# Cross-entropy backward on one core: blocks moved as even and odd partitions instead of row by row

## The chip, the core and the metric

The kernel runs on one core of a Trainium2 chip. The time is device microseconds of one execution; before the change the median of three runs is 1247.4 us (1247.38 to 1247.5).

Of the core, this case uses two compute engines, VectorE (DVE in the profile) and ScalarE (ACT), the queues that SyncE (SP) and ScalarE have for issuing DMAs, and the 16 DMA engines which move the data between the chip's main memory (HBM) and the on-chip memory with its 128 partitions (SBUF). TensorE and GpSimd work for a few microseconds at the start alone.

## The reference

```python
logits: (8, 1024, 8192) float32,  labels: (8, 1024) int32

logits_max = np.max(logits, axis=-1, keepdims=True)
exp_logits = np.exp(logits - logits_max)
softmax = exp_logits / np.sum(exp_logits, axis=-1, keepdims=True)
one_hot[batch_idx, seq_idx, labels] = 1.0
return (softmax - one_hot).astype(np.float32)
```

There are 8192 rows of 8192 numbers. 268 MB are read and 268 MB are written.

## The kernel before, in words

**Tiling.** The 8192 rows are cut into 32 blocks of 256 rows (8 MB). In a block, partition p holds the rows 2p and 2p + 1 of the block, side by side (lines 38 and 39). The two rows of one partition lie next to each other in HBM too: together they are one run of 64 KB, and one of them alone is a run of 32 KB. The code calls the first rows of all partitions j = 0 and the second ones j = 1; "row t" is row j = t % 2 of block t // 2, a tile of 128 partitions x 8192 numbers (4 MB). There are 64 such rows.

**Storage.** The tile X (line 45) has three slots of one block each, 192 KB in each partition. Block b lives in slot b % 3, from its load to its store; all work is done in place. So the load of block b has to wait until block b - 3 is stored.

**Work on a row** (loop of lines 160 to 190). VectorE takes the negated maximum (`row_max`, line 149). ScalarE computes exp(x - max) in place and the sum on the way. VectorE takes the reciprocal of the sum. ScalarE scales the row by it. VectorE subtracts the one-hot, by comparing a row of running numbers with the label (scalar_tensor_tensor, line 186). The order on VectorE is written out by hand: reciprocal of row t, maximum of row t + 1, subtraction of row t. So a row is finished only behind the maximum of the next row, and the last row of a block only after the first maximum of the next block. On ScalarE the order is: exp of row t, the issue of the store of row t - 1 (line 173), scaling of row t. Only the last row of all is scaled and finished in two pieces (lines 175 and 176).

**Transfers.** All loads are issued from SyncE's queue (`load`, line 120), all stores from ScalarE's (`store`, line 132). How a block moves is set by one letter for each block in two strings, LOADS and STORES (lines 13 and 14), and the table PIECES (line 105):

- "r": by row, two DMAs, each on all 128 partitions with runs of 32 KB;
- "w": whole, one DMA on all 128 partitions with runs of 64 KB;
- "h": two DMAs, one on the 64 even partitions and one on the 64 odd ones, both rows, runs of 64 KB.

Each DMA has its own semaphore for its slot and number (lines 58 and 59). A load waits for those stores of block b - 3 that share partitions and rows with it (`meets`, line 111, and line 125). A maximum waits for those loads of its block that have a part of its row (line 151): with "r" one load, with "w" and "h" the whole block. A store is issued with the last row that it holds (line 137): with "r" each row has its own, with "h" both DMAs go out with row j = 1.

Before the change, the loads of blocks 0 to 4 and 26 to 31 are "r" and those of blocks 5 to 25 are "w"; all stores are "r".

All operations are recorded by one helper, `run` (line 63), so the profile shows most of them as line 68.

Of the kernel before, what the change touches and what calls it, by code (L numbers as in the profile page):

```python
# [9 lines left out]
SLOTS = 3  # L10


LOADS = "rrrrrwwwwwwwwwwwwwwwwwwwwwrrrrrr"
STORES = "rrrrrrrrrrrrrrrrrrrrrrrrrrrrrrrr"


@with_exitstack
def kernel(
# [37 lines left out]
    with tc.tile_critical():  # L56
# [63 lines left out]
        def load(b):  # L120
            loaded[b] = []
            before = stored.get(b - SLOTS, last_made if b == SLOTS - 1 else [])
            for q, piece in enumerate(PIECES[LOADS[b]]):
                ps, js = piece
# [7 lines left out]
        def store(t):  # L132
            b, j = divmod(t, G)
            stored.setdefault(b, [])
            for q, piece in enumerate(PIECES[STORES[b]]):
                ps, js = piece
# [88 lines left out]
```

## Time and profile before

| | |
|---|---|
| median of three runs | 1247.4 us (1247.38 to 1247.5) |
| span of the profiled execution | 1245.7 us |
| the profiled execution beyond its span | not in the page; the median lies 1.7 us above the span |
| VectorE busy | 1119.2 us, 90% |
| ScalarE busy | 919.1 us, 74% |
| moved by the DMAs | 536.98 MB, mean 431 GB/s |
| maximum of a row (VectorE) | 64 of 8675 ns |
| subtraction of a row (VectorE) | 63 of 8743 ns |
| exp, and scaling, of a row (ScalarE) | 7123 ns each |
| store of a row, issue to landing | 64, median 30.8 us |
| load of a row, issue to landing | 22, median 26.6 us |
| load of a whole block, issue to landing | 21, median 33.4 us |

The profile is one execution on the chip, as the hardware profiler saw it. It has a page with the busy time of each engine, the span in 40 slices, the DMA queues and the chain of work that ended last, and further views that are asked for one by one: the list of waits, the chain in order of time, the instructions in a stretch of time, the busy times in given windows. Times inside the execution are counted from the start of the span. The trace also has a record for each DMA packet, with its queue, size, start and duration. A packet is one run of a DMA, 32 KB or 64 KB here; each of the 16 engines ends its part of a DMA with a packet of 4 bytes that reports it. A row's DMA gives each engine 8 packets.

In the DMA part, "q1" is the queue of the loads and "q10" that of the stores and of the labels; the columns are packets, MB, and the time that the packets took as a share of 16 engines' span.

### The profile page before, as it was taken

Reading aid. Unit: us, or ns where it says so; the run is one execution under the profiler, and the core shown is the slowest. Engines: PE = TensorE matmul, PEld = TensorE weight load, DVE = VectorE, ACT = ScalarE, POOL = GpSimd, SP = SyncE. Lnnn points to the kernel's source line nnn. Section 1 sums busy time; section 2 is a strip of 40 time slices with the busy share of each in tenths; the row PEclk is TensorE's granted clock in tenths of the full one; section 3 lists DMA queues with packets and bytes.
Section 4 is the critical chain, followed back from the end, with each engine's and each line's share of the span. In section 5 each row is a group of like instructions: output and inputs, shape, how many; then the busy total and the mean of one; then the engine's idle time right before and its main releaser. Section 6 shows DMA issues by size and latency. Waiting matters only on the chain.

```text
span 1245.7 us, 592 instructions
## 1 busy us (share of the span) xinstructions
PE 0.4 (0%) x2; PEld 0.3 (0%) x2; DVE 1119.2 (90%) x196; ACT 919.1 (74%) x194; POOL 7.4 (1%) x7
## 2 busy tenths in 40 slices
PE   0000000000000000000000000000000000000000
PEld 0000000000000000000000000000000000000000
DVE  5999998888988889888998888988889999999893
ACT  3888886778776787767877778777777788887772
POOL 2000000000000000000000000000000000000000
DMA  9999999999999999999999999999999999999998
GB/s 406 417 429 433 438 433 442 437 426 427 430 435 445 439 417 442 426 430 437 432 443 438 420 435 432 430 437 450 420 426 437 436 428 432 437 435 429 432 437 386
DMA packets 15460, 536.98 MB, mean 431 GB/s; under 512 B 1728, under 2 KB 1728, under 8 KB 1760
## 3 DMA queue, kind: packets, MB, share of 16 engines
q1 hardware_dynamic: 6192, 268.44, 50.0%
q10 hardware_dynamic: 9264, 268.51, 49.9%
q14 instruction: 4, 0.03, 0.0%
HBM read 268.50 MB, written 268.44 MB: 431 GB/s over the span
## 4 chain that ended last, share of the span: by engine, by line
DMA 59%; DVE 37%; another core or an unknown queue 2%; ACT 1%; DVEq 0%; issue 0%; PE 0%; SPq 0%; ACTq 0%
DMA X<-in_logits_dram 31%; DMA out_dram<-X 27%; DVE m L68 18%; DVE X L68 18%; ACT X L68 1%; DVE iota L68 0%; DVEq L56 0%; DMA lab_raw<-in_labels_dram 0%; DVE lab_f L68 0%; DVE r L68 0%; PE iota L68 0%; SPq L68 0%; ACTq L68 0%; DVE lab L68 0%
## 5 line engine op out<-in xcount | busy, mean ns | idle before, releaser
L68 DVE TENSOR_REDUCE m<-X 128x1 f32<-128x8192 f32 x64 | 555.2, 8675 | 94.3 <-DMA X<-in_logits_dram 94.3
L68 ACT ACTIVATE X<-X,m 128x8192 f32<-128x8192 f32 x64 | 455.9, 7123 | 188.4 <-DVE m L68 188.4
L68 DVE SCALAR_TENSOR_TENSOR X<-iota,lab,X 128x8192 f32<-128x8192 int16 (+1 forms) x65 | 559.7, 8612 | 4.1 <-ACT X L68 4.1
L68 ACT ACTIVATE X<-X,r 128x8192 f32<-128x8192 f32 (+1 forms) x65 | 456.0, 7017 | 115.9 <-DVE r L68 115.9
L68 DVE RECIPROCAL r<-s 128x1 f32<-128x1 f32 x64 | 9.9, 154 | 7.3 <-ACT X L68 7.3
L68 ACT ACTIVATION_READ_ACCUMULATOR X<-X,m 128x1 f32 x64 | 12.0, 187 | 0.0
L68 DVE CAST lab_f<-lab_raw 32x256 f32<-32x256 int32 x1 | 3.7, 3685 | 4.7 <-DMA lab_raw<-in_labels_dram 4.7
L68 POOL IOTA X<- 128x8192 int16 x1 | 6.9, 6944 | 0.0
L68 DVE TENSOR_SCALAR iota<-X 128x4096 int32<-128x4096 int32 x1 | 4.4, 4427 | 0.1
L68 ACT ACT_TABLE_LOAD x1 | 1.3, 1283 | 1.3 <-SPq L56 1.3
L68 DVE COPY lab<-iota 128x64 f32<-128x64 f32 x1 | 0.2, 225 | 0.5 <-PE iota L68 0.5
L68 PE MATMUL iota<-ident,lab_f 32*128 32x32 f32 x2 | 0.4, 300 | 8.5 <-DVE lab_f L68 8.5
L68 PEld LDWEIGHTS iota<-ident,lab_f 32*128 32x128 f32 x2 | 0.3, 196 | 8.4 <-DVE lab_f L68 8.4
L68 POOL TENSOR_SCALAR_AFFINE_SELECT ident<-ident 32x32 f32<-32x32 f32 x1 | 0.2, 204 | 0.1
L68 POOL MEMSET ident<- 32x32 f32 x1 | 0.1, 115 | 0.5 <-SPq L56 0.5
L209 POOL MEMSET const-bfloat16-1.0<- 128x1 bf16 x1 | 0.1, 107 | 0.0
L209 POOL MEMSET const-uint8-127<- 128x1 uint8 x1 | 0.1, 107 | 0.0
L209 POOL MEMSET const-float32-0.0<- 128x1 f32 x1 | 0.1, 104 | 0.2 <-issue 0.2
L209 POOL MEMSET const-float32-1.0<- 128x1 f32 x1 | 0.1, 104 | 0.0
## 6 DMA issues: line engine op xcount, KB each, us to landing
out_dram<-X ACTq DMA_DIRECT2D x64, 4096.0 KB, 30.8
X<-in_logits_dram SPq DMA_DIRECT2D x22, 4096.0 KB, 26.6
X<-in_logits_dram SPq DMA_DIRECT2D x21, 33.4
lab_raw<-in_labels_dram ACTq DMA_DIRECT2D x1, 64.0 KB, 3.8
```

Source lines behind the costliest of these rows:

```text
L68: instruction = getattr(engine, method)(**operands)
L209: nc = _bacc.Bacc("TRN2", target_bir_lowering=False, num_devices=1)
```

## The change

Two lines change. The loads of blocks 5 to 28 and the stores of blocks 2 to 25 become "h". The load of block b and the store of block b - 3, which use the same slot, are then cut in the same way: the load of the even partitions waits for the store of the even partitions alone, and that of the odd ones for the odd ones alone. The loads of blocks 0 to 4 and 29 to 31 and the stores of blocks 0, 1 and 26 to 31 are "r".

```diff
-LOADS = "rrrrrwwwwwwwwwwwwwwwwwwwwwrrrrrr"
-STORES = "rrrrrrrrrrrrrrrrrrrrrrrrrrrrrrrr"
+LOADS = "rrrrr" + "h" * 24 + "rrr"
+STORES = "rr" + "h" * 24 + "rrrrrr"
```

The functions that read the strings are unchanged. The number of DMAs goes from 43 loads and 64 stores to 64 loads and 64 stores, the bytes stay the same.

## The prediction

> **What bounds the kernel now.** I read the page's second and third parts first: the slices and the DMA queues.
>
> ```profile
> DMA  9999999999999999999999999999999999999998
> GB/s 406 417 429 433 438 433 442 437 426 427 430 435 445 439 417 442 426 430 437 432 443 438 420 435 432 430 437 450 420 426 437 436 428 432 437 435 429 432 437 386
> DMA packets 15460, 536.98 MB, mean 431 GB/s; under 512 B 1728, under 2 KB 1728, under 8 KB 1760
> ...
> q1 hardware_dynamic: 6192, 268.44, 50.0%
> q10 hardware_dynamic: 9264, 268.51, 49.9%
> ```
>
> The 16 DMA engines are busy in every slice, and the two queues (q1 the loads, q10 the stores) add up to 99.9% of 16 engines' span. VectorE (DVE) is at 90%, ScalarE (ACT) at 74%. The windows (us, busy time of PE, PEld, DVE, ACT and POOL, clock, DMA share, GB/s) say the same by stage:
>
> ```profile
> 0.00:46.00 46.00, 0.42 (x2) 0.28 (x2) 33.38 (x7) 22.84 (x6) 7.43 (x7) 1.00 0.97 412
> ...
> 300.00:500.00 200.00, 0.00 (x0) 0.00 (x0) 179.17 (x32) 147.76 (x33) 0.00 (x0) 1.00 1.00 434
> ...
> 1200.00:1246.00 46.00, 0.00 (x0) 0.00 (x0) 26.05 (x5) 19.83 (x5) 0.00 (x0) 1.00 0.92 398
> ```
>
> Only the two ends lose anything: the packet records show data from 2.15 us to 1244.2 us without an idle engine between. The list of waits agrees: VectorE waits for data, not the other way round, and these waits cost nothing by themselves.
>
> ```profile
> DVE m L68 <- DMA X<-in_logits_dram: 94.3, 25, 6.9
> ```
>
> So the time is the length of the packets. The records have one duration for each size, in both queues and at any time after the first microseconds: 1213 ns for 32 KB, 2418 ns for 64 KB, 9 ns for the small packet with which each engine ends a DMA. Each starts where the one before it ends, so no fixed cost hides between them. A 64 KB run is 2 x 1213 - 2418 = 8 ns cheaper than two of 32 KB.
>
> The chain of waits in order of time (start, us, what) shows one turn of the ring of three slots:
>
> ```profile
> 133.53 26.18 DMA out_dram<-X
> 159.71 0.02 issue
> 159.72 32.61 DMA X<-in_logits_dram
> 192.34 0.02 issue
> 192.36 8.69 DVE m L68
> 201.05 8.66 DVE X L68
> 209.71 0.03 DVE r L68
> 209.74 27.34 DMA out_dram<-X
> ```
>
> A store lands, the load into its slot is issued at once, the reduction of the new block starts when all of it is there, and the row before is finished behind that reduction (8.69 + 8.66 = 17.35 us after the landing). The chain shares (DMA 59%, DVE 37%) must not be read as two bounds: while VectorE stands in the chain, the engines are full with other blocks.
>
> **The change part by part.**
>
> 1. Packets. For each engine, before: 64 stores and 22 row loads of 8 packets of 32 KB, 688, and 21 whole loads of 8 packets of 64 KB, 168; 688 x 1.213 + 168 x 2.418 = 1240.8 us. After: 32 row DMAs (10 + 6 loads, 4 + 12 stores) of 8, 256, and 96 half DMAs of 4 packets of 64 KB, 384; 256 x 1.213 + 384 x 2.418 = 1239.0. That is -1.73 us. The queue shares check the size: 49.9% of 16 x 1245.7 over 8192 packets is 1.214 us.
>
> 2. Ending packets. DMAs of X go from 43 + 64 to 64 + 64: 21 more per engine at 9 ns, +0.19 us. Net -1.54 us.
>
> 3. Length of a packet that serves every second partition. The trace has no DMA on 64 partitions. Nothing below: the 8 ns are all that is fixed in a packet, so 384 packets can save at most another 3.1 us. Above, the nearest row in size is the whole load, 2.418 us, always. The only DMA on fewer partitions is that of the labels (32, packets of 2 KB: 81 to 315 ns, median 98), but the first packets of X on 128 partitions beside it are stretched as well (1.37 to 2.11 us for 1.213), so it shows the start and no price of partitions. I take 2.418.
>
> The row to weigh is that 128-partition DMAs keep 434 GB/s and both queues share them packet by packet. [...]
>
> 4. Stores wait for both rows of their block. The store of an even row is issued 17.3 us later than now, behind the odd row. It costs nothing if the queues hold other work, which is the open question; see the walk below.
>
> 5. Loads wait for half a block. Block b's even half needs only the even half of block b - 3 stored; now a whole load waits for both rows. Behind that wait on SP stand only the odd half's load and later loads, whose own stores land later anyway.
>
> 6. ACT issues two stores back to back, 0.34 us each, at every second row, ahead of the scaling activation. That one now ends about 1 us before VectorE takes its result (47.39 + 7.12 = 54.51, next operation 55.52), so 0.34 us more is hidden; uncovered, it would be 24 x 0.34 = 8 us of VectorE, which itself waits 94 us.
>
> **Walk through one block.** A half is 4 packets an engine, 9.67 us alone. The walk asks whether both queues are ever empty. When the even half of the store lands, the odd half goes on alone until the first packet of the new even load; from landing to that packet the records have 4.1 to 5.4 us, so about two odd packets pass. Then load and store alternate, and the ending packet of the odd store takes a turn too: when it goes out, the even load has at least one packet, 2.42 us, to run. The odd load needs 0.36 us from the last packet to the landing and 1.19 us from issue to first packet on an idle engine (issue at 0.96, data at 2.15): 1.55 us, inside the 2.42. Then the odd load runs, and the next block's stores arrive: VectorE needs 34.6 us a block, the DMAs 38.7 us, so VectorE again settles at waiting some 4 us in each block for data (94.3 / 25 = 3.8 now), behind full queues. The bandwidth stays whole, with less in hand than now, where the store queue always holds a row more.
>
> The two ends. The fourth store, the last by row, lands at 127.9 us, and the first half store is issued at 133.5 (behind the sixth row, where now the sixth row store is issued); block 4's second row, 9.7 us by itself, is loaded in between. At the tail:
>
> ```profile
> 1199.76 8.69 DVE L68 TENSOR_REDUCE m<-X 128x1 f32<-128x8192 f32 x1 [1.93 <-DMA X<-in_logits_dram]
> ...
> 1217.14 0.34 ACTq L68 DMA_DIRECT2D out_dram<-X  x1
> 1221.27 8.88 DVE L68 SCALAR_TENSOR_TENSOR X<-iota,lab,X 128x4096 f32<-128x4096 int16 x2 [4.09 <-ACT X L68]
> 1230.18 0.34 ACTq L68 DMA_DIRECT2D out_dram<-X  x1
> ```
>
> The last store is issued 30.4 us after the last load has landed, and its first packet leaves 2.4 us later, behind the stores before it. The last three blocks still move by row in both queues, the last load still waits for the store six rows back, so about three and a half rows of stores (34 us) are left then; if it were three (29.1 us), 2.5 us would be lost.
>
> **Sum.** 1245.7 - 1.54 = 1244.2 us for the profiled execution. The median lies 1.7 us above the span, so 1245.9 us, 0.12% less. What a measurement of this kernel can tell from no change is about 0.2%, 2.5 us.
>
> **Rivals.**
>
> A. The queues stay full: 1245.9. Speaks for it: the walk, and the excess of 4 us per block that VectorE has. Chance 0.60.
>
> B. The ring runs dry once per block (slower). Place: between the end of the even load and the first packet of the odd one. It decides when the even load's remainder is shorter than 1.55 us, or the engines are apart by a packet. Price: up to 1.55 us in each of 24 blocks, 37 us, 1283. For it: the store queue has no spare row any more, and store and load now wait for each other in pieces of 9.67 us. Against it: the 2.42 us remainder. Chance 0.18, mostly over 2.5 us.
>
> [...] Chance 0.14; most of it stands outside my range.
>
> D. The change does not do what it says: stores leave as 32 KB packets in spite of 64 KB runs (only loads show 64 KB now). Then 3 more blocks of loads save 24 x 8 ns, the ending packets take it back: 1247.4. Chance 0.05.
>
> E. Over 0.2% faster: there is only the fixed part of the packets to gain (3.1 us more at most), 1242.8. Chance 0.03.
>
> **Numbers.** Faster 0.03 (E); same 0.65 (A and D); slower 0.32 (B and C). The range goes from E's 1242.8 to the end of B, 1283.5, and leaves out C, 0.14.
>
> **What would show it.** Right: 6144 packets in q1 and 6192 in q10 (6144 of X, 48 of the labels), 2418 ns for a 64 KB store packet, DMA share 1.00 from 46 to 1200 us, VectorE's wait for data again near 95 us, now in about 24 waits. B shows as windows at 0.95 to 0.98 with VectorE's waits grown by the same time. [...] D shows in the packet count. Wrong altogether: if the tail's last store is issued to an empty queue, or if the bytes per second rise above 436 in the middle.

## The result and the profile after

The changed kernel takes 1282.67 us (median; 1281.23 to 1288.46) against 1247.45 us for the kernel before in the same runs. The ratio is 1.029, interval 1.026 to 1.031: 2.9% slower, where 0.1% faster was forecast. The profiled execution has a span of 1280.3 us, 34.6 more than before. The page of the changed kernel, its slices and queues as they were shown of before:

```profile
DMA  9999999999999999999999999999999999999998
GB/s 404 417 433 435 407 426 367 450 430 394 426 414 438 426 393 448 395 434 426 414 434 397 426 426 409 428 397 434 428 394 426 393 436 444 418 424 437 428 440 380
DMA packets 12340, 536.98 MB, mean 419 GB/s; under 512 B 2064, under 2 KB 2064, under 8 KB 2096
...
q1 hardware_dynamic: 6144, 268.44, 50.5%
q10 hardware_dynamic: 6192, 268.51, 48.6%
```

The DMAs are the forecast ones: 6144 and 6192 packets. The busy digits say nothing new, every slice but the last a 9. The rate does: between the ends it falls to 367 to 397 GB/s in eight slices. The windows (the last two columns are DMA share and GB/s):

```profile
159.00:300.00 141.00, 0.00 (x0) 0.00 (x0) 119.89 (x22) 97.88 (x21) 0.00 (x0) 1.00 0.98 409
300.00:500.00 200.00, 0.00 (x0) 0.00 (x0) 177.91 (x32) 147.19 (x32) 0.00 (x0) 1.00 1.00 422
500.00:700.00 200.00, 0.00 (x0) 0.00 (x0) 170.10 (x30) 139.51 (x30) 0.00 (x0) 1.00 0.99 416
700.00:900.00 200.00, 0.00 (x0) 0.00 (x0) 175.89 (x32) 144.91 (x32) 0.00 (x0) 1.00 0.99 419
```

The share is nearly full while 3 to 6% of the rate is gone (434, 433 and 436 GB/s before in these windows). So most of the loss is packets that count as busy and last longer. A packet record shows when a packet begins and ends; summed over all packets behind the first 10 us and divided by 16, the time beyond 2418 ns in the 64 KB load packets is 23.0 us (0.6 before). Idle engines account for 9.0 us (0.2 before), 64 KB store packets for 1.9, 32 KB load packets for 3.2 (1.2 before). That is 22.4 + 8.8 + 1.9 + 2.0 = 35.1 us, less the 1.5 saved in packets 33.6; the data end 34.6 us later than before (1278.7 for 1244.2).

Most of the lost time comes in 11 places, 80 us apart, one for every two blocks. They hold 21.9 us of the long load packets and 8.5 us of the idle time. Outside them the largest single piece is 1.5 us of long packets at 130 to 138 us. The first places are at 211 and 291 us:

```profile
200.00:220.00 20.00, 0.00 (x0) 0.00 (x0) 20.00 (x4) 12.76 (x3) 0.00 (x0) 1.00 0.94 364
220.00:240.00 20.00, 0.00 (x0) 0.00 (x0) 18.14 (x4) 15.92 (x4) 0.00 (x0) 1.00 0.98 423
...
280.00:300.00 20.00, 0.00 (x0) 0.00 (x0) 20.00 (x4) 12.08 (x3) 0.00 (x0) 1.00 0.98 380
```

What surrounds the first of them, from the chain of waits in order of time (start, us, what):

```profile
170.14 0.02 issue
170.16 25.72 DMA X<-in_logits_dram
195.88 0.02 issue
195.91 8.69 DVE m L68
204.59 7.32 DVE X L68
211.91 1.25 issue
213.17 0.17 DVE r L68
213.33 0.43 ACTq L68
213.76 0.04 issue
213.80 37.91 DMA out_dram<-X
```

The odd load of block 5 lands at 195.88, and block 4 is finished behind the reduction that waited for it; its two stores go out at 213.28 and 213.80. By the packet records and landings, the odd store of block 3 has landed at 211.31 by then and the even load of block 6 has run its data on most engines by 210.2 (median). The store queue has nothing more until 219. The odd load of block 6 is issued at 211.33, behind that landing, and its first packets begin at 212.7 (median). From there its packets take 3.1 and then 3.6 us (medians; 3.9 at most), until the new stores enter at 219. In this first place the engines are idle for 2.4 us on average, since one engine ended its part of the store 2.8 us behind the others; in the later ones it is 0.2 to 1.4 us (as a small one: even load's data out at 291.9, odd load's first packet at 292.2), and the long packets come all the same.

VectorE again waits for data, 24 times as forecast, with 108.6 us for the forecast 95. The second line is new, and the last was 4.1 us before:

```profile
DVE m L68 <- DMA X<-in_logits_dram: 108.6, 24, 9.2
ACT X L68 <- issue: 86.2, 24, 5.2
ACT X L68 <- DVE r L68: 67.5, 40, 2.1
DVE X L68 <- ACT X L68: 23.0, 13, 4.1
```

ScalarE now spends more time in issuing: a store of 64 partitions takes 0.48 us to issue, the second of a pair 0.6 to 0.8 or, in every second block, 1.4 to 3.2 us (0.34 before). All store issues take 54 us, 22 before. The 86.2 us are more than what the issues add, since they take in waits for the reciprocal that stood in the third line before (115.9 us then): both lines together grew by 37.8 us.

These holds don't make the stores late. VectorE finishes the last row of a block behind the first maximum of the next one, which waits for the next block's odd load. In all 22 blocks from 4 to 25 the first store of the pair is issued 17.40 us after that load has landed (213.28 after 195.88, 293.62 after 276.22). That is the maximum, 8.69 us, and the subtraction, 8.66, with nothing left for ScalarE.

### The profile page after: what moved, and what is told of

Read it like the earlier page. It is cut to its first block, busy times and chain, and to the rows that moved or that the text cites. A ratio compares the mean times of both kernels' runs of the same rounds, so it can differ in the third digit from the quotient of the medians.

```text
span 1280.3 us, 640 instructions
## 1 busy us (share of the span) xinstructions
PE 0.4 (0%) x2; PEld 0.3 (0%) x2; DVE 1120.5 (88%) x196; ACT 917.7 (72%) x194; POOL 7.4 (1%) x7
## 3 DMA queue, kind: packets, MB, share of 16 engines
q1 hardware_dynamic: 6144, 268.44, 50.5%
q10 hardware_dynamic: 6192, 268.51, 48.6%
## 4 chain that ended last, share of the span: by engine, by line
DMA 64%; DVE 32%; issue 1%; ACT 1%; ACTq 0%; DVEq 0%; PE 0%; SPq 0%
DMA out_dram<-X 39%; DMA X<-in_logits_dram 25%; DVE m L68 16%; DVE X L68 14%; ACT X L68 1%; ACTq L68 0%; DVE iota L68 0%; DVEq L56 0%; DVE lab_f L68 0%; DMA lab_raw<-in_labels_dram 0%; DVE r L68 0%; PE iota L68 0%; DVE lab L68 0%; ACTq L220 0%; DVEq L67 0%
## 5 line engine op out<-in xcount | busy, mean ns | idle before, releaser
L68 DVE TENSOR_REDUCE m<-X 128x1 f32<-128x8192 f32 x64 | 555.1, 8674 | 108.6 <-DMA X<-in_logits_dram 108.6
L68 ACT ACTIVATE X<-X,r 128x8192 f32<-128x8192 f32 (+1 forms) x65 | 456.0, 7016 | 153.7 <-issue 86.2
L68 ACT ACT_TABLE_LOAD x1 | 1.3, 1283 | 1.4 <-SPq L56 1.4
```

The lines of the kernel that those rows point to most:

```text
L68: instruction = getattr(engine, method)(**operands)
```

## The experiments

Three theories: **ring** (a block's stores go out only behind its second row, so both queues run empty together), **partitions** (packets on every second partition are longer), **issue** (the paired store issues hold ScalarE). The excess is the time beyond the usual packet length (2418 ns) in 64 KB load packets, an engine; idle is that of the engines before the last DMA begins.

| run | median us | ratio, interval | excess | idle |
|---|---|---|---|---|
| the change | 1282.7 | 1.029 [1.026, 1.031] | 23.0 | 9.0 |
| h loads, row stores | 1253.6 | 1.005 [1.003, 1.006] | 2.1 | 4.8 |
| whole loads, h stores | 1367.1 | 1.095 [1.094, 1.097] | 48.3 | 67.9 |
| whole loads, whole stores | 1341.2 | 1.075 [1.073, 1.076] | 43.3 | 51.5 |
| the change, short subtraction | 1273.9 | 1.020 [1.019, 1.022] | 11.6 | 4.5 |
| h loads to block 25, row stores | 1250.9 | 1.002 [1.001, 1.003] | 2.1 | 0.7 |
| the same, quarter stores | 1271.1 | 1.019 [1.017, 1.021] | 12.3 | 9.5 |
| before, stores held | 1331.6 | 1.067 [1.065, 1.069] | 41.3 | 41.8 |

**One part alone: the loads.**

```diff
-STORES = "rr" + "h" * 24 + "rrrrrr"
+STORES = "r" * 32
```

> Three theories. Ring: the stores of a block go out only behind its second row, so the store queue keeps no row in hand, both queues run empty together, and the loop store, load, reduction, store sets the pace. Partitions: DMAs on every second partition have longer packets (the excess over 2418 ns sums to 23 us an engine in the loads and 2 us in the stores). Issue: two stores issued back to back hold ScalarE (86 us of issue waits). This kernel loads as even and odd partitions and stores every block by row. Ring: 1247 us, within 3 us of before. Partitions: about 1270, as the loads carry nearly all the excess. Issue: 1247.

Measured: 1253.6. Nearly all long load packets are gone though the loads still use every second partition; the middle of the run has no idle time. The 4.8 us of idle stand at the end, where the last load lands at 1204 us and VectorE, still behind, begins its row at 1209. Ring is 3 us off its range, partitions 16 us; issue gave the same 1247 as ring.

**The other part alone: the stores.**

```diff
-LOADS = "rrrrr" + "h" * 24 + "rrr"
+LOADS = "rrrrr" + "w" * 24 + "rrr"
```

> Whole loads (128 partitions) for blocks 5 to 28, stores as in the change (even and odd partitions). Ring: as slow as the change or slower, 1283 to 1320, since a whole load waits for both halves of the store. Partitions: only the stores' 2 us of excess, about 1249. Issue: about 1283, the doubled issues stay.

Measured: 1367.1, beyond even the upper end that ring gave. Here no store issue takes more than 0.63 us, so ScalarE is not held as in the change, and the kernel is 84 us slower than the change: long issues aren't needed for the loss.

**Late stores without any half.**

```diff
-LOADS = "rrrrr" + "h" * 24 + "rrr"
-STORES = "rr" + "h" * 24 + "rrrrrr"
+LOADS = "rrrrr" + "w" * 24 + "rrr"
+STORES = "rr" + "w" * 24 + "rrrrrr"
```

> The same blocks, loads and stores each as one DMA on all 128 partitions with runs of 64 KB; stores still behind the second row. Ring: slow, 1283 to 1330, the granules are larger. Partitions: about 1246, no DMA on half of the partitions is left. Issue: about 1246, one store issue in a block.

Measured: 1341.2. Every DMA has 128 partitions and a block has one store issue, and still the long packets sum to nearly twice those of the change. The partitions theory falls here as the cause of the long packets, and issue misses by 95 us. Halves in both queues, the change, are 58 us faster than this. Half stores beside whole loads are 26 us slower than it, which no run explains.

**The decisive one: before, with nothing changed but when the even rows' stores are issued.**

```diff
-                if js.stop != j + 1:
+                if 2 <= b < 26 and j == 0:
+                    continue
+                if not 2 <= b < 26 and js.stop != j + 1:
                     continue
```

(The store of row j = 1 then issues both rows' DMAs.)

> The kernel before, and only the issue of the even rows' stores of blocks 2 to 25 is held until the odd row is finished too; all DMAs keep their 128 partitions, their sizes and their number. Ring: this alone makes it slow, near the 1341 of whole loads and whole stores (1320 to 1345). Partitions: 1247. Issue: two issues back to back as in the change, on 128 partitions, at 0.34 us each, so about 1250.

Measured: 1331.6, 6.7% slower, within ring's range. Sizes, partitions and number of DMAs are those of before, and the issues stay at 0.5 us or less. The windows of this run against 434 and 433 GB/s before:

```profile
300.00:500.00 200.00, 0.00 (x0) 0.00 (x0) 160.38 (x29) 132.76 (x29) 0.00 (x0) 1.00 0.96 396
500.00:700.00 200.00, 0.00 (x0) 0.00 (x0) 163.54 (x29) 140.16 (x30) 0.00 (x0) 1.00 0.95 392
```

The excess and the idle time account for it: 40.7 + 41.6 + 0.9 = 83.2 us, where the data end 83.5 us later. So holding the stores is enough to make long packets and idle engines, with no half and no long issue.

The same can be read over all runs, from the issues and landings between 200 and 900 us. In the kernel before, and in the three runs in which a row's store goes out as soon as the row is done, some store is on its way at every moment. There is none for 3.5% of that time in the change (1.9% with the short subtraction), for 12.6% in this run, and for 17.9 and 21.5% in the two whole-load runs. The run with quarter stores, below, doesn't fit: it is slow with a store always on its way.

**Shorter work between load and store.**

```diff
+            if t + 1 < T:
+                cols = [slice(0, V // 2)]
             for c, w in zip(cols, scaled):
```

> The change as it is, but the subtraction of the one-hot covers only the first 4096 columns of each row but the last (the other half of the one-hot is left out), so VectorE needs 4.3 us less for a row and a block's store follows 13.1 us after the next block's landing instead of 17.35. The packets and DMAs are those of the change. Ring: the loop of two blocks loses more than its excess, 1246 to 1250. Partitions: 1283, nothing changes. Issue: between, about 1265, the holds on ScalarE stay but VectorE has more slack.

Measured: 1273.9, 9 us less than the change, a miss for all three numbers. The stores go out 13.13 us behind the landing in all blocks from 6 to 25, as planned, so the issues delay nothing here either. VectorE waits 200 us for data now, and still 11.6 us of excess in the load packets, 10.6 in the store packets and 4.5 of idle remain. So the stretch behind VectorE is not the whole loss. That the rest comes from the two queues waiting for each other half by half is an argument, and no run shows it.

**Back to the old tail, and halves by row.**

```diff
-LOADS = "rrrrr" + "h" * 24 + "rrr"
-STORES = "rr" + "h" * 24 + "rrrrrr"
+LOADS = "rrrrr" + "h" * 21 + "rrrrrr"
+STORES = "r" * 32
```

> Loads as even and odd partitions for blocks 5 to 25 alone, row by row from block 26 on as before the change; all stores by row. The run with h loads to block 28 and stores by row lost 4.8 us, all at the end, where VectorE was still working off rows when the last load had landed. Ring: with six blocks of row loads ahead of the end VectorE has caught up, the packets are those of before plus 21 endings: 1247.5 us. Partitions: over 1250, since 21 blocks of loads still use every second partition.

Measured: 1250.9, ratio 1.002. The idle time at the end is gone (0.7 us), as ring has it, but the time is 3.4 us over ring's and within what partitions gave. Some 3 us stay, in small pieces (1.5 us of excess in 64 KB loads, 0.8 in other loads, 0.7 in stores, 0.5 idle). A small price of every second partition isn't excluded by this, and nothing was gained by the halves.

```diff
+            "q": [(slice(i, P, 2), slice(j, j + 1)) for j in range(G) for i in range(2)],
...
-STORES = "r" * 32
+STORES = "rr" + "q" * 21 + "r" * 9
```

> As the run before, and the stores of blocks 2 to 22 also go by every second partition, but still row by row (four DMAs of 2 MB in a block, runs of 32 KB), so each row leaves as soon as it is done. Ring: the stores are in time, the queue keeps its rows: 1247 to 1250. Partitions: load and store both on every second partition as in the change, 1275 to 1285. Issue: two issues for every row, more than in the change, 1285 or more.

Measured: 1271.1. This one fits none of the three: it misses ring's range and issue's, and lies below that of partitions. Its 32 KB store packets last 1213 ns as ever (0.4 us of excess in all), so they aren't longer for their partitions. The waits again show issues:

```profile
ACT X L68 <- issue: 150.4, 42, 5.6
...
DVE X L68 <- ACT X L68: 4.1, 1, 4.1
```

The second issue of a pair takes 0.9 to 3.6 us at even rows (j = 0) from block 3 on, and all store issues take 93 us. But the stores aren't late by it: the first issue of every pair comes 0.03 us behind its subtraction, and VectorE's waits for ScalarE are those of before, 4.1 us, and 7.3 on its first row. What the records show is that from about 560 us on the store queue is nearly, but never quite, empty once in each block, and that the load packets beside it are long (0.6 to 1.0 us each time). At the end 7 us are idle. So cutting the stores by partitions costs 20 us against the run before it though they go out in time, and why stays open.

**What a dry spell costs.** Three streams of loads with no computation (other outputs left out) and one row's store entering at every second block; these and the two runs behind them were executed once each:

```diff
-LOADS = "rrrrr" + "h" * 24 + "rrr"
+LOADS = "h" * 32
...
+            load(b)
+            if b % 2 == 0 or b == B - 1:
+                arrived = [w for _, w in loaded[b]]
+                w = run(nc.scalar, arrived, put[b % SLOTS][0], "dma_start", ...)
```

> A stream of loads (even and odd partitions, all 32 blocks) with no computation; one row of every second block and of the last is stored as it was loaded, so 17 single stores come into an empty store queue while the load queue is full; the outputs are left out but for these rows. Packets: 256 x 2.418 + 17 x 8 x 1.213 = 784 us, ends some 6 us. If the long load packets are the price of a store that comes into an empty queue (some 1.9 us an engine each), 16 of them add 30 us: about 820, and the long packets stand ahead of each store. If they are the price of starting all 16 engines from idle, no long packets: 790. If they are due to every second partition, long packets at any time, over 830.

> The stream of loads again, whole blocks on 128 partitions, same 17 single stores, outputs left out as before. Partitions: 790 us and no long packet while the stream by even and odd partitions has them. Entry into an empty store queue: the same as that stream, about 820 us.

> The stream of loads by row (128 partitions, runs of 32 KB), same 17 single stores, outputs left out as before. Packets: 512 x 1.213 + 136 x 1.213 = 786 us. Entry into an empty store queue: the price goes with the packet size, about 1.2 us each, so 786 + 20 + 6 = 812. Without such a price 792.

Measured: 792.3 us by halves, 798.3 whole, 794.4 by row, with an excess of 0.8, 4.8 and 1.9 us. The stream by even and odd partitions, in two windows:

```profile
100.00:300.00 200.00, 0.00 (x0) 0.00 (x0) 0.00 (x0) 0.00 (x0) 1.00 1.01 435
300.00:500.00 200.00, 0.00 (x0) 0.00 (x0) 0.00 (x0) 0.00 (x0) 1.00 1.01 435
```

435 GB/s: these DMAs on every second partition lose nothing against the kernel before, which moves 433 to 436 GB/s in its windows from 159 to 900 us. The time is the 790 us that was given for a price of starts alone, not the 820 for a price of each entering store: here, with several loads queued, the first store that enters stretches the load packets ahead of it by 0.8 us an engine, and the other 16 cost nothing. Then the load stream with a dry spell before each block, without and with a store that enters later:

```diff
-                free = [w for other, w in before if meets(piece, other)]
+                free = [w for other, w in before if meets(piece, other)] + held
...
+            load(b)
+            held = [w for _, w in loaded[b]]
+            if b > 0:
+                w = run(nc.scalar, held[:1], put[(b - 1) % SLOTS][0], "dma_start", ...)
+                held.append(w)
```

(The run without stores has not the last three lines; it stores one row at the end.)

> Loads alone, as even and odd partitions, each block issued only when the block before has landed, so the engines start from idle 31 times; no computation, one row stored at the end, all other outputs left out. Packets: 256 x 2.418 + 9.7 = 629 us; idle 1.55 each, 48. If a start from idle stretches the first packets by 0.75 us and the second by 1.1, as in the change, 57 us of excess more: 735. If only the entry of a store stretches packets, 680 and no excess.

> The same starts from idle, and in each block one row's store (of the block before, as it was loaded) is issued when the even half has landed, so that it enters an empty store queue while the odd half is running alone; the other outputs are left out. Packets: 256 x 2.418 + 31 x 9.7 = 920, idle 48. If starts alone stretch packets: the same excess as without stores. If the entry of a store stretches them: 1.1 to 1.9 us more for each of the 31 stores, 34 to 59 us of excess beyond that of the run without stores.

Measured: 726.6 and 1070.4 us. Without stores the excess is 20.7 us, nearly all of it in the first packet of each start, 3080 ns on average for 2418: 0.66 us for each of 31 starts, beside 70.9 / 31 = 2.3 us of idle. With stores it is 61.7, so 41.0 / 31 = 1.32 us more for each store, in the last packets ahead of the store's first (3460 ns for the seventh of eight). A start and an entry, 0.66 + 1.32 = 1.98 us, for 11 dry spells are 21.8 us: the change has 21.9 in these places.

## Why the prediction was wrong, point by point

Packets and endings (steps 1 and 2) were right: 6144 and 6192, 2418 ns for a 64 KB store packet too.

Packets on every second partition (step 3): the value taken, 2418, was right. The longer ones in the change aren't due to the partitions, since whole loads have more of them (43.3 and 48.3 us for 23.0) and the stream of halves has 0.8 us of them in all. The streams show no loss of rate for even and odd partitions: 435 GB/s by halves, 430 to 432 in whole blocks. The 0.14 for C was the chance of such longer packets.

The stores behind both rows (step 4) were costed at nothing by the **walk through one block**, and that is the step that failed. It set 2.42 us of even load still to run against 1.55 us until the odd load's first packet, and concluded that the engines never lack work. In the eleven dry spells the even load's data ended (median of the engines) only 0.2 to 1.7 us after the last engine's ending packet of the odd store (291.9 after 290.4, 371.8 after 370.3; in the first spell 0.8 us before it), and the odd load's first packet came 1.7 to 2.2 us after it (292.2, 372.3). So the cover is short by 0.2 to 1.6 us, and by 2.5 in the first spell, where one engine lags. The second part of the walk failed in the same place and cost more: "then the odd load runs, and the next block's stores arrive". They do, but after the load has begun alone on engines that ran dry, and what was not in the walk is that such a start and such an entry make packets longer, 1.98 us together. In the blocks between (a spell in every second block) the next stores were issued before the odd store had landed, at 249.87 for 251.71, and nothing was lost.

A like price stood in the trace of before, against the prediction's reading that packets have one duration at any time after the first microseconds. From 48.7 to 52.4 us, just ahead of the first store, two 32 KB load packets on each engine take 1.4 to 2.3 us for 1.213, 1.17 us an engine in all. That is the one place in that trace, past its start, where a store enters an empty store queue.

The halves in step 5 work as said, and better than whole loads, by 84 us beside half stores. Step 6 was mis-sized: 0.48 and 0.6 us, or 1.4 to 3.2, for the 0.34 taken from 128-partition rows. VectorE waits 18.9 us more for ScalarE, but in each of the 12 blocks with a long second issue it then waits 6.8 to 9.2 us for data (1.7 us up to 178.5, then 8.6 up to 195.9), so these holds don't reach the stores.

The tail held: the last store is issued at 1264.8 us and follows the one before it without a gap.

Rival B named the place and, at 1283, the time. But it came out so by compensation: 11 dry spells instead of 24, and each dearer, (21.9 + 8.5) / 11 = 2.8 us instead of 1.55, since the long packets were not in its price; the rest of the loss lies outside these places. That its time came so near is luck. It deserved more than 0.18: the trace of before showed that the store queue was the one that always had work (between 200 and 900 us the load queue has 18 stretches of 10.2 to 11.4 us without a packet, the store queue none over 4.2 us), and the change took away just that. The sign that was named for B, a DMA share of 0.95 to 0.98, showed only in part (0.98 to 1.00), because stretched packets count as busy (1.00 at 422 GB/s from 300 to 500 us, for 1.00 at 434 before); VectorE's waits for data grew by 14 us, not by the whole loss.

What stays open: when an entering store stretches the packets ahead of it. It cost 1.32 us where few loads were queued after a start from idle, but also 1.17 us in the kernel before and 1.5 at 138 us in the change, where the engines had not been idle, and nothing for 16 of 17 stores in the full stream of halves. Open too is why the second issue of a pair takes 1.4 us or more in some blocks, and why stores cut by partitions cost 20 us though they go out in time. That last cost may have a share in the change's loss outside its dry spells, and perhaps in them. No version here beats the kernel before.

## What to carry to other kernels

In this kernel the DMA engines were the bound and always busy (99.9% of 16 engines' span). What larger runs could gain there was the fixed part of a packet, 8 ns (2 x 1213 - 2418); what could be lost was the backlog that kept them busy. Before a transfer is merged, ask when its first part was issued until now: holding the even rows' stores for one row's time, 17 us, cost 6.7% with every DMA otherwise as it was. Read GB/s beside the DMA share: here a share of 1.00 stood beside 422 GB/s in the change and 434 before, since packets lasted longer.

## What the runs showed of the hardware that was not expected

- The first 64 KB packet after all engines were idle took 3.08 us for 2.42 (mean of 31 starts, loads from idle without stores). The load packets just ahead of a store that entered an empty store queue were at times stretched too: 3.6 us for 2.42 in the first dry spell of the change, 3.46 in the run of starts with stores, and 1.4 to 2.3 for 1.213 in the kernel before.
- The DMAs on 64 partitions in the change took longer to issue than those on 128 in the kernel before: 0.48 us for 0.34 on ScalarE's queue and 0.47 for 0.33 on SyncE's. The second of a pair on ScalarE's took up to 3.2 us, and with quarter stores 0.9 to 3.6 us.
- 64 KB loads on every second partition streamed at 435 GB/s, whole blocks on all 128 at 430 to 432.
